# A key's decay to its block's end by a scan from the right, and the scores in two matmuls per chunk

## The chip, the cores and the metric

The kernel runs on one core of a Trainium2 chip. Its time is the device time of one execution, in microseconds: the median of three runs is 2411.07 us (2410.68 to 2414.14). The profiled execution took 2410.45 us, of which the trace spans 2408.7 us.

## The reference

One decoder layer over a prompt of 2048 tokens with 16 meta tokens ahead of it, and over 8 sample sequences of one token each. Half of the mixing width is a gated linear recurrence with four heads of 128 keys and 128 values, the other half a 31-tap depthwise convolution; a squared-ReLU MLP follows. What the change touches is the recurrence of the prompt, computed chunk by chunk:

```
b = jnp.cumsum(logf, axis=3)          # log of the gates, summed from the block's start
b_end = b[:, :, :, -1:, :]
q_dec = q * jnp.exp(b)
k_inv = k * jnp.exp(-b)               # divided by the decay from the block's start
k_end = k * jnp.exp(b_end - b)        # decay from the key to the block's end
scores = jnp.where(causal, einsum('bnhtd,bnhsd->bnhts', q_dec, k_inv), 0.0)
o_intra = einsum('bnhts,bnhsv->bnhtv', scores, v)
ds = einsum('bnhsd,bnhsv->nbhdv', k_end, v)
s_next = exp(b_end) * s + ds ;  o = o_intra + einsum(q_dec, s)
```

## The kernel before

The prompt is worked through in four quarters (q = 0 to 3) of 512 tokens; quarter 0 also carries the 16 meta tokens and the 8 sample tokens. Phase 1 is a list of units, each one 128-column piece of a weight matrix times the quarter's activations: 24 input units per quarter ("in": per head the gate f, the query q, the output gate g and the value v, and the pairs a, b of the convolution) and 8 output units ("out"). A unit of quarter 0 is 48 matmuls of 260 or 268 columns, of the other quarters 24 of 512. Each product is three matmuls of high and low parts (mm3, L645). Phase 2 is the MLP, in two halves of the tokens. TensorE (PE) runs the units one after the other; a unit's epilogue (in_epilogue, L1270) takes its result out of PSUM. In quarter 0 that is a VectorE multiply by a row of norms, so a unit can start only when the epilogue of the unit two before it has freed its banks.

Everything else is background work, written as generators that a planner interleaves with the units (Background, L159). The planner keeps a model of each engine's time (Proxy, L112: a scan costs 60 + 3.0 ns per element, a reciprocal 75 + 6.4, a tensor-tensor operation 155 + 1.045) and lets a step be written into its engine's queue once the model says that its inputs are ready; a VectorE step may be written when the engine's model is less than 600 ns ahead (HORIZON, L160). All that stands between two `yield` lines is written in one go. The order that results is fixed when the program is built, and each engine then follows its queue.

The background work that matters here is `hgrn` (L887), once per quarter and head, 16 times in all, one at a time (hgate). It works on four chunks of 128 tokens, each of two blocks of 64. A forward scan makes B, the decay from each block's start; the reciprocal of all of B makes I; keys times I, times the first block's decay, give the key operand K of the scores and, times the second block's decay, the operand I of the state update. QS, Q and K are the operands of the score matmuls; the tile scT takes the masked scores; vn and KPn are the transposed values and keys; Sch and Sst hold the states. KPn is used again for the normed output, whose transposes end the head's work on PE. Other background work beside it: the convolution's taps (conv_part, L1092; a tap is a VectorE operation on a PSUM bank, or a ScalarE multiply and a GpSimd add), the preparation of the next quarter's inputs (x_pair, L393; row_bc, L370, its broadcast through the tile dg), the sample rows' convolution (conv_sample, L1134) and state update (hgrn_sample, L1018). All instructions carry line 154, that of the helper which records them, so groups are read by their tiles.

Of the kernel before, what the change touches and what calls it, by code (L numbers as in the profile page):

```python
# [13 lines left out]
ALU = mybir.AluOpType  # L14
AX = mybir.AxisListType

P = 128
# [4 lines left out]
QT = SEQ // NQ  # L22
META = 16
# [204 lines left out]
def tile_hybrid_step(  # L228
# [6 lines left out]
    V, S, G, T, SP = (Proxy(e, n, model) for e, n in (  # L235
        (nc.vector, "dve"), (nc.scalar, "act"), (nc.gpsimd, "pool"), (nc.tensor, "pe"), (nc.sync, "dma")))
# [45 lines left out]
    ps = psum.tile([P, 8, 512], F32, name="ps")  # L282
# [18 lines left out]
    def keep(n):  # L301

        if kcols[0] + n > 88:
            kcols[0] = 0
        a = kept[:, kcols[0]:kcols[0] + n]
        kcols[0] += n
        return a
# [34 lines left out]
    def bank1():  # L342
        got = yield from bank(1)
        return got[0]
# [441 lines left out]
    with tc.manual_schedule():  # L786
# [4 lines left out]
        with ExitStack() as p1:  # L791
            mix_p = p1.enter_context(tc.tile_pool(name="mix", bufs=1))

            def mt(shape, name, dt=F32):
                return mix_p.tile(shape, dt, name=name)
# [7 lines left out]
                     for t, n in (("F", 2), ("K", 2), ("Q", 2), ("Sg", 4), ("V", 2))}  # L803
            B_t = mt([P, QT + META], "B")
            I_t = mt([P, QT + META], "I")
            d1 = mt([P, QT], "d1")
            QS = mt([P, 4, P], "QS")
            vn = mt([P, 4, P], "vn")
            KPn = mt([P, 4, P], "KPn")
# [77 lines left out]
            def hgrn(q, h, tl):  # L887
                Ft, Kt, Qt, Sg, Vt = tl["F"], tl["K"], tl["Q"], tl["Sg"], tl["V"]
                yield from take1(hgate)
                p0 = META if q == 0 else 0  # L890
                Fp = Ft[:, p0:p0 + QT]
                Bp = B_t[:, p0:p0 + QT]
                Ip = I_t[:, p0:p0 + QT]
                Kp, Qp = Kt[:, p0:p0 + QT], Qt[:, p0:p0 + QT]
                yield "dve"
                V.tensor_copy(d1[:, 0:QT:64], Fp[:, 0:QT:64])
                V.memset(Fp[:, 0:QT:64], 0.0)
                V.tensor_tensor_scan(Bp, Fp, d1, 0.0, ALU.mult, ALU.add)
                if q == 0:
                    V.tensor_tensor_scan(B_t[:, 0:META], Ft[:, 0:META], mone, 1.0, ALU.mult, ALU.mult)  # L900
                n = p0 + QT
                V.reciprocal(I_t[:, 0:n], B_t[:, 0:n])
                yield "pe"
                bv = yield from bank1()
                for j in range(4):
# [6 lines left out]
                def pr(t):  # L912
                    return t.rearrange("p (j u t) -> p j u t", j=4, u=2)

                kv, qv, iv, bvw = pr(Kp), pr(Qp), pr(Ip), pr(Bp)
                EA = bvw[:, :, 0, 63:64]
                EB = bvw[:, :, 1, 63:64]
                EAb = EA.to_broadcast([P, 4, 64])
                EE, IA = keep(4), keep(4)
                V.tensor_tensor(Kp, Kp, Ip, ALU.mult)  # L920
                V.tensor_copy(IA, iv[:, :, 0, 63])
                V.tensor_tensor(kv[:, :, 0], kv[:, :, 0], EAb, ALU.mult)
                if q == 0:
                    V.scalar_tensor_tensor(out=Kt[:, 0:META], in0=Kt[:, 0:META], scalar=B_t[:, META - 1:META],
                                           in1=I_t[:, 0:META], op0=ALU.mult, op1=ALU.mult)
                V.tensor_tensor(Ip.rearrange("p (j t) -> p j t", j=4), Kp.rearrange("p (j t) -> p j t", j=4),
                                EB.to_broadcast([P, 4, P]), ALU.mult)
                yield "dve"
                V.tensor_tensor(EE, EA.rearrange("p j o -> p (j o)"), EB.rearrange("p j o -> p (j o)"), ALU.mult)
                V.tensor_tensor(qv[:, :, 0], qv[:, :, 0], bvw[:, :, 0], ALU.mult)  # L930
                V.tensor_tensor(QS[:, :, 64:P], qv[:, :, 1], bvw[:, :, 1], ALU.mult)
                V.tensor_tensor(QS[:, :, 0:64], qv[:, :, 0], IA.unsqueeze(2).to_broadcast([P, 4, 64]), ALU.mult)
                V.tensor_tensor(qv[:, :, 1], QS[:, :, 64:P], EAb, ALU.mult)
                yield "pe"
                bk = yield from bank1()
# [13 lines left out]
                bs = yield from bank1()  # L949
                for j in range(4):  # L950
                    T.matmul(ps[:, bs, j * P:(j + 1) * P], lhsT=Kp[:, j * P:(j + 1) * P], rhs=QS[:, j],
                             start=True, stop=True)
                yield "dve"
                V.copy_predicated(scT, mask.unsqueeze(1).to_broadcast([P, 4, P]),
                                  ps[:, bs, :].rearrange("p (j t) -> p j t", j=4))
# [314 lines left out]
            def in_epilogue(u, q, t, c):  # L1270
# [31 lines left out]
                else:  # L1302
# [17 lines left out]
                    if t == "v":  # L1320
                        bg.add(hgrn(q, c, dict(cur)), 2)
                        if q == 0 and c == HEADS - 1:
                            bg.add(hgrn_sample_norm(), 1.7)
# [76 lines left out]
            for u in range(2, n_phase1):  # L1400
                kind, q, t, c, pi = plan[u]
# [308 lines left out]
```

## Time and profile before

| | us |
|---|---|
| median of three runs | 2411.07 |
| profiled execution | 2410.45 |
| its span in the trace | 2408.7 |
| PE busy | 2343.8 (97%) |
| VectorE (DVE) busy | 1086.2 (45%) |
| ScalarE (ACT) busy | 685.7 (28%) |
| GpSimd (POOL) busy | 579.1 (24%) |

PE is busy nearly all of the span, and its waits are short; 45% for VectorE is a mean over phase 1, where it is nearly full in places, and phase 2, where it is nearly idle. So the averages say little on what a change inside phase 1 is worth: that is read from the waits of PE, and from stretches of 25 us, whose PE clock column says what part of the full clock (2.4 GHz) the engine was granted; a stretch below 1.00 holds some time at 1.2 GHz.

### The profile page before, as it was taken

Reading aid. Unit: us, or ns where it says so; the run is one execution under the profiler, and the core shown is the slowest. Engines: PE = TensorE matmul, PEld = TensorE weight load, DVE = VectorE, ACT = ScalarE, POOL = GpSimd, SP = SyncE. Lnnn points to the kernel's source line nnn. Section 1 sums busy time; section 2 is a strip of 40 time slices with the busy share of each in tenths; the row PEclk is TensorE's granted clock in tenths of the full one; section 3 lists DMA queues with packets and bytes.
Section 4 is the critical chain, followed back from the end, with each engine's and each line's share of the span. In section 5 each row is a group of like instructions: output and inputs, shape, how many; then the busy total and the mean of one; then the engine's idle time right before and its main releaser. Section 6 shows DMA issues by size and latency. Waiting matters only on the chain.

```text
span 2408.7 us, 31153 instructions
## 1 busy us (share of the span) xinstructions
PE 2343.8 (97%) x13000; PEld 2097.1 (87%) x13000; DVE 1086.2 (45%) x1454; ACT 685.7 (28%) x1244; POOL 579.1 (24%) x383
## 2 busy tenths in 40 slices
PE   8988899999999989999999999999999999999998
PEld 8987788978888878999999999999888888888887
DVE  6887968478469342522323323325422222222224
ACT  6544645454355232211211211213200100100112
POOL 4653525455256023222222222211000000000000
PEclk9998999999999999999999999999999999999999
DMA  9774555944654668444444444449522222222222
GB/s 309 232 231 140 175 192 189 319 158 174 232 197 168 213 226 302 149 136 149 140 132 144 144 131 140 146 135 338 186 105 88 97 96 88 105 88 104 89 89 104
DMA packets 159218, 396.25 MB, mean 165 GB/s; under 512 B 8772, under 2 KB 107657, under 8 KB 125278
## 3 DMA queue, kind: packets, MB, share of 16 engines
q1 hardware_dynamic: 158934, 394.00, 48.1%
q8 instruction: 102, 1.67, 0.3%
q14 instruction: 38, 0.31, 0.0%
q10 hardware_dynamic: 144, 0.26, 0.0%
HBM read 265.91 MB, written 128.79 MB: 164 GB/s over the span
## 4 chain that ended last, share of the span: by engine, by line
PE 78%; DVE 4%; issue 1%; ACT 1%; POOL 1%; DMA 0%; POOLq 0%; ACTq 0%; DVEq 0%
PE ps L154 78%; DVE ps L154 2%; DVE I L154 1%; DVE act L154 1%; POOL scr L154 0%; DMA wsp<-kw 0%; ACT scr L154 0%; DVE kept L154 0%; DVE B L154 0%; DVE K L154 0%; DVE scr L154 0%; DVE stat L154 0%; DVE QS L154 0%; DVE d L154 0%; ACT F L154 0%
## 5 line engine op out<-in xcount | busy, mean ns | idle before, releaser
L154 PE MATMUL ps<-act,wsp 128*128 128x512 f32 (+5 forms) x7704 | 1502.6, 354 | 13.4 <-DVE F L154 9.3
L154 PEld LDWEIGHTS ps<-act,wsp 128*128 128x128 f32 x7704 | 1284.3, 191 | 174.5 <-DVE F L154 7.1
L154 PE MATMUL ps<-hid,wsp 128*128 128x344 f32 (+4 forms) x3864 | 713.9, 346 | 0.9 <-DMA wsp<-kw 0.9
L154 PEld LDWEIGHTS ps<-hid,wsp 128*128 128x128 f32 x3864 | 646.5, 188 | 63.4 <-DVE kept L154 0.7
L154 POOL TENSOR_TENSOR wsp<-raw,wsp 128x1024 fp32r<-128x1024 f32 (+1 forms) x98 | 234.9, 2396 | 630.0 <-ACT wsp L154 579.5
L154 DVE TENSOR_TENSOR acc<-ps,acc 128x1032 f32<-128x1032 f32 (+5 forms) x160 | 162.1, 1013 | 470.4 <-PE ps L154 470.3
L154 DVE TENSOR_TENSOR xn<-xn 128x1032 f32<-128x1032 f32 (+3 forms) x68 | 79.9, 1176 | 520.7 <-ACT hid L154 520.7
L154 ACT ACTIVATE xn<-ps 128x1032 f32<-128x1032 f32 (+5 forms) x74 | 69.2, 935 | 849.6 <-PE ps L154 846.9
L154 POOL TENSOR_TENSOR scr<-scr 128x512 f32<-128x512 f32 x177 | 239.5, 1353 | 148.5 <-ACT scr L154 131.2
L154 POOL TENSOR_TENSOR kept<-stat,mhalf 128x4 f32<-128x4 f32 (+4 forms) x48 | 38.5, 804 | 900.8 <-DVE stat L154 900.2
L154 DVE SCALAR_TENSOR_TENSOR ps<-glu,cw,ps 128x512 f32<-128x512 f32 x287 | 216.1, 753 | 8.0
L154 ACT ACTIVATE wsp<-raw 128x1024 fp32r<-128x1024 f32 (+1 forms) x98 | 101.5, 1036 | 298.2 <-PE ps L154 222.3
L154 DVE TENSOR_TENSOR hid<-xn,hid 128x1032 fp32r<-128x1032 f32 (+3 forms) x68 | 135.5, 1993 | 2.3
L154 ACT ACTIVATE scr<-glu,cw 128x512 f32<-128x512 f32 x193 | 129.0, 714 | 0.5 <-DVE glu L154 0.5
L154 ACT ACTIVATE junk<-ps 128x128 bf16<-128x128 f32 (+3 forms) x100 | 38.3, 383 | 121.0 <-PE ps L154 105.2
L154 DVE TENSOR_TENSOR scr<-ps,scr 128x512 f32<-128x512 f32 x48 | 32.8, 684 | 85.3 <-DMA scr<-xscr 60.8
L154 ACT ACTIVATE hid<-xn 128x1032 fp32r<-128x1032 f32 (+3 forms) x68 | 69.0, 1015 | 2.2
L154 POOL TENSOR_TENSOR fg<-fg 128x512 f32<-128x512 f32 x28 | 37.7, 1346 | 82.1 <-ACT fg L154 82.1
L154 DVE RECIPROCAL I<-B 128x512 f32<-128x512 f32 (+1 forms) x16 | 54.0, 3378 | 0.5
L154 DVE TENSOR_TENSOR act<-scr,act 128x512 fp32r<-128x512 f32 (+1 forms) x31 | 27.8, 897 | 46.1 <-ACT act L154 46.1
L154 ACT ACTIVATE scr<-ps,vec 128x128 f32<-128x128 f32 (+1 forms) x68 | 25.3, 454 | 28.3 <-PE ps L154 28.3
L154 ACT ACTIVATE fg<-scr 128x512 f32<-128x512 f32 x32 | 20.0, 628 | 45.2 <-DVE scr L154 41.6
(185 smaller groups left out, 1139.7 us busy)
## 6 DMA issues: line engine op xcount, KB each, us to landing
wsp<-kw SPq DMA_DIRECT2D x167, 1024.0 KB, 4.8
kw<-wsp SPq DMA_DIRECT2D x96, 1024.0 KB, 5.7
raw<-in_w_up_dram SPq DMA_DIRECT2D x32, 512.0 KB, 6.4
raw<-in_w_down_dram SPq DMA_DIRECT2D x32, 512.0 KB, 6.0
raw<-in_w_in_dram SPq DMA_DIRECT2D x24, 512.0 KB, 8.0
out_dram<-xn SPq DMA_DIRECT2D x18, 512.0 KB, 4.6
scr<-xscr SPq DMA_DIRECT2D x32, 256.0 KB, 7.0
hscr<-scr SPq DMA_DIRECT2D x32, 256.0 KB, 6.4
```

Source lines behind the costliest of these rows:

```text
L154: return fn(*args, **kw)
```

## The change

The reciprocal of whole rows is gone. Instead a second scan runs over the gates from the right and puts into I the decay from each key to its own block's end (the tile d1, one column longer, restarts it with ones at each block's end). The keys of the first block times that are the first half of K; the keys of the second block times that go into the second half of I; the first half of I is the first half of K times the second block's decay. Only the eight decays at the block ends are inverted (IE), and quarter 0's 16 meta tokens. The second half of K now holds bare keys until a new multiply overwrites it with QS times the inverse decay of the second block, as a query operand. A chunk's scores are then two matmuls: the one of 128 by 128 as before, and behind it one of 64 by 64 that writes the second block's scores over the lower right quarter. A `yield "dve"` stands between the two scans. The planner's costs are as before.

```diff
-            d1 = mt([P, QT], "d1")
+            d1 = mt([P, QT + 1], "d1")
...
-                V.tensor_tensor_scan(Bp, Fp, d1, 0.0, ALU.mult, ALU.add)
+                V.tensor_tensor_scan(Bp, Fp, d1[:, 0:QT], 0.0, ALU.mult, ALU.add)
+                yield "dve"
+                V.memset(d1[:, 64:QT + 1:64], 1.0)
+                V.tensor_tensor_scan(Ip[:, ::-1], Ft[:, p0 + 1:p0 + QT + 1][:, ::-1], d1[:, 1:QT + 1][:, ::-1], 0.0,
+                                     ALU.mult, ALU.add)
                 if q == 0:
                     V.tensor_tensor_scan(B_t[:, 0:META], Ft[:, 0:META], mone, 1.0, ALU.mult, ALU.mult)
-                n = p0 + QT
-                V.reciprocal(I_t[:, 0:n], B_t[:, 0:n])
+                    V.reciprocal(I_t[:, 0:META], B_t[:, 0:META])
...
-                EE, IA = keep(4), keep(4)
-                V.tensor_tensor(Kp, Kp, Ip, ALU.mult)
-                V.tensor_copy(IA, iv[:, :, 0, 63])
-                V.tensor_tensor(kv[:, :, 0], kv[:, :, 0], EAb, ALU.mult)
+                EE, IE = keep(4), keep(8)
+                V.tensor_tensor(kv[:, :, 0], kv[:, :, 0], iv[:, :, 0], ALU.mult)
+                V.tensor_tensor(iv[:, :, 1], kv[:, :, 1], iv[:, :, 1], ALU.mult)
...
-                V.tensor_tensor(Ip.rearrange("p (j t) -> p j t", j=4), Kp.rearrange("p (j t) -> p j t", j=4),
-                                EB.to_broadcast([P, 4, P]), ALU.mult)
+                V.tensor_tensor(iv[:, :, 0], kv[:, :, 0], EB.to_broadcast([P, 4, 64]), ALU.mult)
                 yield "dve"
+                V.reciprocal(IE, Bp[:, 63:QT:64])
                 V.tensor_tensor(EE, EA.rearrange("p j o -> p (j o)"), EB.rearrange("p j o -> p (j o)"), ALU.mult)
+                ie = IE.rearrange("p (j u) -> p j u", u=2)
                 V.tensor_tensor(qv[:, :, 0], qv[:, :, 0], bvw[:, :, 0], ALU.mult)
                 V.tensor_tensor(QS[:, :, 64:P], qv[:, :, 1], bvw[:, :, 1], ALU.mult)
-                V.tensor_tensor(QS[:, :, 0:64], qv[:, :, 0], IA.unsqueeze(2).to_broadcast([P, 4, 64]), ALU.mult)
+                V.tensor_tensor(QS[:, :, 0:64], qv[:, :, 0], ie[:, :, 0:1].to_broadcast([P, 4, 64]), ALU.mult)
+                V.tensor_tensor(kv[:, :, 1], QS[:, :, 64:P], ie[:, :, 1:2].to_broadcast([P, 4, 64]), ALU.mult)
                 V.tensor_tensor(qv[:, :, 1], QS[:, :, 64:P], EAb, ALU.mult)
...
                     T.matmul(ps[:, bs, j * P:(j + 1) * P], lhsT=Kp[:, j * P:(j + 1) * P], rhs=QS[:, j],
                              start=True, stop=True)
+                    T.matmul(ps[64:P, bs, j * P + 64:(j + 1) * P], lhsT=iv[:, j, 1],
+                             rhs=kv[:, j, 1], start=True, stop=True)
```

Since the planner's model sees other costs, the order of all of phase 1 behind the first scan changes with it. Three places follow, in the order in which the engines' queues hold the instructions.

The first is VectorE at the first head of quarter 0. F_115 is that head's gate, F_116 the next head's, whose row is the epilogue that frees PSUM for a unit of PE; rows `ps<-glu,cw,ps` are taps of the convolution. Before:

```order
L154 COPY d_129<-F_115 128x8
L154 MEMSET F_115 128x8 [waits DVE_49]
L154 SCALAR_TENSOR_TENSOR B<-F_115,d_129 128x512 [waits DVE_49]
L154 SCALAR_TENSOR_TENSOR B<-F_115,ones 128x16
L154 RECIPROCAL I<-B 128x528 [waits DVE_49]
L154 TENSOR_TENSOR F_116<-ps,fg 128x536 [waits PE_49]
```

Now:

```order
L154 COPY d_129<-F_115 128x8
L154 MEMSET F_115 128x8 [waits DVE_49]
L154 SCALAR_TENSOR_TENSOR B<-F_115,d_129 128x512 [waits DVE_49]
L154 MEMSET d_129 128x8 [waits DVE_49]
L154 SCALAR_TENSOR_TENSOR I<-F_115,d_129 128x512 [waits DVE_49]
L154 SCALAR_TENSOR_TENSOR B<-F_115,ones 128x16
L154 RECIPROCAL I<-B 128x16 [waits DVE_49]
L154 TENSOR_TENSOR F_116<-ps,fg 128x536 [waits PE_49]
```

The epilogue keeps its place behind the scans; the long reciprocal ahead of it has become a memset, a second scan and a reciprocal of 16 columns.

The second is VectorE at the second head of quarter 0, where `xn<-xn,cw` and `aux<-xn` are the sample rows' convolution, scT the head's masked scores and Sch and Sst its states. Before:

```order
L154 COPY xn_91<-glu 128x8
L154 TENSOR_TENSOR xn_91<-xn_91,cw 128x248 [waits DVE_49,Activation_49]
L154 TENSOR_REDUCE aux<-xn_91 128x8 [waits DVE_49]
L154 TENSOR_TENSOR aux<-aux,vec 128x32 [waits DVE_49]
L154 SCALAR_TENSOR_TENSOR ps<-glu,cw,ps 128x512
L154 COPY_PREDICATED scT<-mask,ps 128x512 [waits PE_49]
L154 SCALAR_TENSOR_TENSOR ps<-glu,cw,ps 128x512 [waits DVE_49] x5
L154 SCALAR_TENSOR_TENSOR Sch<-Sch,kept,ps 128x128 [waits Activation_49]
```

Now:

```order
L154 SCALAR_TENSOR_TENSOR ps<-glu,cw,ps 128x512 [waits DVE_49] x6
L154 COPY_PREDICATED scT<-mask,ps 128x512 [waits PE_49,Activation_49]
L154 SCALAR_TENSOR_TENSOR ps<-glu,cw,ps 128x512 [waits DVE_49] x3
L154 TENSOR_TENSOR Sg_123<-ps,fg 128x520 [waits DMAHW0_49,PE_49]
L154 SCALAR_TENSOR_TENSOR xn_90<-xn_91,smp,xn_90 128x128 [waits DMAHW3_49,DMAHW6_49,DMAHW2_49,Activation_49]
L154 SCALAR_TENSOR_TENSOR xn_90<-xn_91,smp,xn_90 128x128 [waits Activation_49] x7
L154 SCALAR_TENSOR_TENSOR Sch<-Sch,kept,ps 128x128 [waits PE_49,Activation_49]
L154 SCALAR_TENSOR_TENSOR Sch<-Sch,kept,ps 128x128 [waits DVE_49] x2
L154 SCALAR_TENSOR_TENSOR Sst<-Sch,kept,ps 128x128 [waits DVE_49]
L154 COPY xn_93<-glu 128x8 [waits DMAHW1_49]
L154 TENSOR_TENSOR xn_93<-xn_93,cw 128x248 [waits DVE_49]
L154 TENSOR_REDUCE aux<-xn_93 128x8 [waits DVE_49]
```

The sample rows' convolution, four rounds of copy, multiply and reduce, stood ahead of scT and now stands behind the head's states; six taps stand ahead of scT.

The third is PE at the first head's scores. Before:

```order
L154 MATMUL ps<-act,wsp_87 128x268 x18
L154 MATMUL ps<-act,wsp_88 128x268 x4
L154 MATMUL ps<-act,wsp_88 128x268 [waits Pool_49]
L154 MATMUL ps<-act,wsp_88 128x268
L154 MATMUL ps<-QS,K_117 128x128 [waits Activation_49]
L154 MATMUL ps<-QS,K_117 128x128 x3
```

Now:

```order
L154 MATMUL ps<-act,wsp_89 128x268
L154 MATMUL ps<-ident,V_125 16x128
L154 MATMUL ps<-ident,K_117 16x128
L154 MATMUL ps<-act,wsp_89 128x268 x24
L154 MATMUL ps<-QS,K_117 128x128 [waits DVE_49]
L154 MATMUL ps<-K_117,I 64x64
```

The head's scores stand in an earlier unit (wsp_89 here is the value unit of the second head, wsp_87 and wsp_88 the units a and b that come after it), and a 64x64 matmul follows each of the four.

## Rows read from the trace of the kernel before

**Rows 1.** The page: engines over the span; the clock in 40 slices, tenths.

```profile
PE 2343.8 (97%) x13000; PEld 2097.1 (87%) x13000; DVE 1086.2 (45%) x1454; ACT 685.7 (28%) x1244; POOL 579.1 (24%) x383
...
PEclk9998999999999999999999999999999999999999
```

**Rows 2.** Stretches of 25 us: busy us (instructions) per engine, PE clock, DMA share, GB/s.

```profile
75.00:100.00 25.00, 20.80 (x150) 20.10 (x150) 23.53 (x29) 10.57 (x16) 13.71 (x9) 0.86 0.62 187
...
150.00:175.00 25.00, 23.55 (x178) 23.23 (x177) 20.47 (x22) 14.37 (x25) 17.73 (x11) 0.90 0.56 174
175.00:200.00 25.00, 14.03 (x71) 12.74 (x70) 24.02 (x45) 9.40 (x33) 10.01 (x7) 0.66 0.47 147
200.00:225.00 25.00, 22.04 (x155) 21.07 (x154) 20.21 (x29) 11.25 (x19) 10.48 (x8) 0.93 0.51 181
...
575.00:600.00 25.00, 25.00 (x114) 20.37 (x113) 24.04 (x35) 13.19 (x24) 13.48 (x11) 1.00 0.54 203
```

**Rows 3.** Waits of PE by the engine waited for: us in total, times, longest.

```profile
PE ps L154 <- ACT KPn L154: 12.0, 3, 9.1
PE ps L154 <- DVE F L154: 9.3, 3, 3.7
PE ps L154 <- DVE scT L154: 7.5, 2, 7.2
```

**Rows 4.** Timeline, quarter 0, first head: start, us, instruction, [idle before it, releaser].

```profile
76.49 3.10 POOL L154 TENSOR_TENSOR wsp<-raw,wsp 128x1024 fp32r<-128x1024 f32 x1 [0.16 <-ACT wsp L154]
77.33 2.31 DVE L154 TENSOR_TENSOR_SCAN B<-F,ones 128x16 f32<-128x16 f32 x1
...
79.67 3.45 DVE L154 RECIPROCAL I<-B 128x528 f32<-128x528 f32 x1
...
83.04 0.65 DVE L154 TENSOR_TENSOR F<-ps,fg 128x536 f32<-128x536 f32 x1
...
83.84 1.64 PE L154 MATMUL ps<-act,wsp 128*128 128x260 f32 x6 [2.64 <-DVE F L154]
```

**Rows 5.** Timeline, VectorE, the first head of quarter 1, which nothing disturbs.

```profile
304.24 1.23 DVE L154 TENSOR_TENSOR_SCAN B<-F,d 128x512 f32<-128x512 f32 x1
...
305.50 3.35 DVE L154 RECIPROCAL I<-B 128x512 f32<-128x512 f32 x1
...
310.32 0.69 DVE L154 TENSOR_TENSOR I<-K,B 128x512 f32<-128x512 f32 x1
310.93 0.16 DVE L154 TENSOR_TENSOR kept<-B 128x4 f32<-128x4 f32 x1
311.00 0.42 DVE L154 TENSOR_TENSOR Q<-Q,B 128x256 f32<-128x256 f32 x1
...
311.34 0.42 DVE L154 TENSOR_TENSOR QS<-Q,B 128x256 f32<-128x256 f32 x1
```

**Rows 6.** Timeline, PE: narrow and full matmuls; a record is one pass.

```profile
280.61 0.60 PE L154 MATMUL ps<-ident,aux 128*8 128x128 f32 x4
281.04 1.06 PE L154 MATMUL ps<-QS,K 128*128 128x128 f32 x8
281.86 0.47 PE L154 MATMUL ps<-act,wsp 128*128 128x512 f32 x1
...
285.70 0.48 PE L154 MATMUL ps<-small 16*128 16x128 f32 x2
...
330.83 1.84 PE L154 MATMUL ps<-smp,xn 128*128 128x2 f32 x16
...
476.89 0.73 PE L154 MATMUL ps<-ones,fg 128*128 128x2 f32 x17
```

**Rows 7.** Timeline, quarter 0, second head: the scores and what follows them.

```profile
170.96 1.13 PE L154 MATMUL ps<-QS,K 128*128 128x128 f32 x8 [1.45 <-DVE QS L154]
...
182.05 0.71 DVE L154 COPY_PREDICATED scT<-mask,ps 128x512 f32<-128x512 int32 x1
...
182.82 0.79 PE L154 MATMUL ps<-small 16*128 16x128 f32 x2 [7.18 <-DVE scT L154]
```

## The prediction

> **What bounds the kernel now.** I read the page first. PE is busy for 97% of the span and its clock is full in nearly every slice [rows 1], so time can be won or lost in three ways: matmuls that PE has more or fewer of, waits of PE, and the stretches in which it is granted 1.2 instead of 2.4 GHz. The list of PE's waits came next: the three largest entries that the change can touch are 12.0 us for KPn, 9.3 us in three waits for F, and 7.5 us for scT [rows 3]. The stretches of 25 us say where: in quarter 0 PE is busy 20.80, 23.55, 14.03 and 22.04 of 25 us, at clocks of 0.86, 0.90, 0.66 and 0.93. At 575 us, with the later quarters, it is busy 25.00 of 25 at a clock of 1.00, while VectorE is busy 24.04 [rows 2]. So the change is decided in quarter 0, some 75 to 310 us. In the later quarters whatever VectorE gains or loses is hidden by PE, which has no wait there to give back. The timeline last, to see what each wait stands behind.
>
> **The change part by part.** The sum starts from the profiled run, 2410.45 us (2408.7 in the span and 1.75 around it); the median is 0.6 us above.
>
> *VectorE's work per head.* Removed: the reciprocal, keys times I, the copy, the decay of the first half and the 512-wide I, which together run from 305.50 to 310.93 in an undisturbed head, 5.43 us. Added: a scan like the first (304.24 to 305.50, 1.26 us), four multiplies of 256 columns at 0.34 (311.00 to 311.34), a memset and a reciprocal of eight columns. The last two are not in the trace; the smallest operation takes a slot of 0.07 us (310.93 to 311.00) and a duration of 0.16, so 0.3 for both [rows 5]. Together 2.9, or 2.5 us less per head and 40 us over 16 heads. Twelve of the heads lie in the later quarters under PE's full stretches and count as nothing; if that cover were gone, each would be worth at most its 2.5 us. A scan that reads from right to left is not in the trace either; I take the forward one's 1.26, and as bounds that and the reciprocal's 3.35 [rows 5]. At 3.35 the gain of the next two items is gone.
>
> *The waits for F, −6.3 us.* In quarter 0 the next head's gate must leave PSUM before PE can start the unit two further on. That copy stands behind everything that the recurrence writes into VectorE's queue in one go: at the first head behind the reciprocal, from 79.67 until the copy's 83.04, 3.37 us, and PE waits 2.64 [rows 4]. The order of the changed kernel leaves the copy there, but the 3.37 become a memset, a scan and a reciprocal of 16 columns, 0.1 + 1.26 + 0.1: the copy comes 1.9 us sooner. At the third head the order puts it between the two scans, so that it waits for less still. Three waits of 9.3 in all [rows 3], the first of 2.64, the longest 3.7: each loses 1.9, at most what it is, so 5.7 if all lose the same and up to 7.5 where one goes altogether; I take 6.3 and keep 0 and 9.3 as ends.
>
> *The clock, −6 us.* Each of the three waits falls into a stretch with a lower clock: 0.86, 0.90 and 0.93 of 25 us are 3.5, 2.5 and 1.75 us of lost PE work [rows 2]. A wait of 1.45 us cost nothing of the kind: the eight passes behind it took 1.13 us against 1.06 in a stretch without a wait [rows 6, 7]. What remains of the F waits is 0.7 to 1.8 us. Of the 7.75 I take 6; the ends are 0 and 7.75.
>
> *The second score matmul, +10.0 us.* 64 matmuls (four chunks, 16 heads), each of two passes as the old ones (128 records for 64 matmuls). The trace has no 64x64. A full pass takes 0.10 to 0.11 us: eight begin at 281.04 and the next work at 281.86. A pass of 128 weight columns with only two moving columns still takes 0.115 (1.84 over 16); one of eight weight columns and two moving, 0.043 (0.73 over 17) [rows 6]. So wide weights cost as much as wide data, and half of both should take half, 0.056. Behind the two short passes the next chunk's 128 weight columns are only half covered, 0.055 more, for three of four chunks. That is 64 x 2 x 0.056 + 48 x 0.055 = 9.8, taken as 10. PE is the bound, so all of it counts. Ends: 128 x 0.043 = 5.5, and 128 x 0.24 = 30.7 with the dearest narrow pass, that of 16 rows (0.48 over two) [rows 6].
>
> The Trainium skill has a rule against this part: TensorEngine Tiling (Array Packing), section Tiling Modes, says that changing the tiling mode, not merely the tile, drains TensorE. By it each of the 64 would cost as the third rival has it; the eight-column transposes, which are narrow tiles too, show no such drain.
>
> *The second head's scores, −5 us.* PE waits 7.18 us at the meta tokens' product because the masked copy into scT only ran at 182.05, behind the sample rows' convolution on VectorE [rows 7]. That stretch has the lowest clock, 0.66, or 8.5 us lost [rows 2]. In the changed order the convolution stands behind the head's states; ahead of scT are six taps, at 0.75 to 0.8 each some 4.6 us, against about 5 us of PE work, so a wait of 2 to 4 us may stay. That is −4 in waits and about −4 in clock. Against it: at the first head the broadcast rows for the next inputs (tile dg) now come behind the masked copy, and the head's steps on PE stand closer together; I put +3 for new waits there. The ends are wide, since an order has no times: −17 (7.18 and 8.5 and a little) to +9 (as much new waiting as the F waits are now).
>
> *What stays.* The longest wait for KPn, 9.1 us [rows 3], belongs to the last head of quarter 0, whose norm waits for taps on VectorE and adds on GpSimd. The new order has six taps and a conv start ahead of that step, where six taps and a small subtraction stood, and nearly the same work of PE; I leave it as it is. Behind the end of phase 1 PE's order is the old one.
>
> The sum: 2410.45 + 10.0 − 6.3 − 6 − 5 = 2403.2, so 2403 us, 0.3% below the median.
>
> **Rivals.** *Waits merely change their place* (25%). The F waits and their clock go, and the new order makes as many waits as it removes: 2410.45 + 10 − 12.3 = 2408, no change that can be told. For it: the planner's costs did not change, and what makes PE wait in quarter 0 is that they do not know of delays such as the next rival's. Against it: the worst wait has a cause, the sample rows' convolution, that leaves its place.
>
> *The second scan is held up by GpSimd* (9%), slower. A scan of 16 columns took 2.31 us: it began at 77.33 and ended at 79.64, just behind a GpSimd subtraction that ended at 79.59 [rows 4]. The reciprocal kept its usual time. If every new scan in quarter 0 is held for as long, 2.2 us, then 0.1 + 1.26 + 2.2 + 0.1 is 3.7 and no shorter than the reciprocal; F waits and clock stay, the head's steps come as late as before and the new order gains nothing: 2410.45 + 10 = 2420. It decides from a mean hold of 1.9 us. Against it: GpSimd is busy in only half of that stretch (13.71 of 25) [rows 2].
>
> The Trainium skill states this, SBUF — State Buffer, section Who interferes with whom: a VectorE instruction with two SBUF inputs contends with a GpSimd one that reads SBUF, one with a single input does not, and the loser blocks for the whole instruction. The 2.31 us agree. By that rule the change trades a single-input reciprocal for two-input scans and multiplies.
>
> *The narrow matmul is dear* (8%), slower: each switch between 128 and 64 columns empties PE, so that a pass costs the 0.24 us of the 16-row product [rows 6]: 30.7 in place of 10, 2424. Against it: four transposes with eight weight columns run from 280.61 to 281.04, 0.11 each, with no gap on either side.
>
> *Quarter 0 comes out nearly free of waits* (14%): in addition to the forecast, the second head loses its whole 7.18 and 8.5 and no new wait arises at the first: 2410.45 + 10 − 12.3 − 16 = 2392.
>
> That the change does not do what it says can be left out: the order shows the reciprocal gone and 64 matmuls more.
>
> **How the numbers follow.** Forecast 44%, own range 2396 to 2410; rivals 25, 9, 8 and 14%. Range 2388 to 2420: below, the last rival with a matmul at its lower end; above, the hold of the scan; the dear matmul lies outside. About 0.2%, 5 us, is what a measurement of this kernel tells from no change: faster is below 2406, slower above 2416. Faster: 38 of the forecast's 44, 14 of the last rival, 5 of the second-named 25 (the case of moved waits), 57%. Same: 6 of the forecast, 17 of the moved waits, 2 of the held scan, 25%. Slower: 3 of the moved waits, 7 of the held scan, 8 of the dear matmul, 18%.
>
> **What would show it.** In the profile after: no RECIPROCAL of 512 columns; 16 more scans of 1.2 to 1.4 us; VectorE some 35 to 40 us less busy; PE's wait for F below 4 us in total; clocks in the stretches from 75 to 225 us nearer to 1; scT no longer among PE's long waits; KPn still with one of about 9; 128 records of 64x64 with 0.05 to 0.12 us from one to the next; PE some 10 us busier. The prediction is wrong if F still costs 9 us, if a pass of 64 takes over 0.2 us, or if new waits of 10 us or more stand in quarter 0.

## The result and the profile after

| | before | after |
|---|---|---|
| median, us | 2409.73 (2408.32 to 2414.14, 6 runs) | 2428.18 (2425.84 to 2429.98, 6 runs) |
| profiled execution, us | 2410.45 | 2427.06 |
| PE busy, us | 2343.8 | 2366.4 |
| VectorE busy, us | 1086.2 | 1045.3 |
| PE's waits, sum of the list, us | 56.6 | 50.3 |

The ratio is 1.0074 (95% interval 1.0061 to 1.0087): the changed kernel is slower by 18 us where 7 us less were forecast. Three things have to be read off: VectorE did get lighter by 41 us, PE waits 6 us less, and PE itself works longer.

First the engines, the line of the page that answers to [rows 1].

```profile
PE 2366.4 (98%) x13128; PEld 2110.1 (87%) x13128; DVE 1045.3 (43%) x1494; ACT 684.4 (28%) x1240; POOL 578.0 (24%) x379
```

Next the stretches of 25 us, with the columns of [rows 2], and behind those the two in which something went wrong that was not foreseen.

```profile
75.00:100.00 25.00, 21.54 (x160) 20.22 (x160) 23.41 (x34) 10.87 (x16) 17.15 (x11) 0.93 0.67 204
150.00:175.00 25.00, 23.97 (x179) 22.77 (x179) 22.06 (x37) 12.20 (x33) 13.76 (x9) 0.93 0.62 208
175.00:200.00 25.00, 18.01 (x121) 17.28 (x120) 23.00 (x37) 12.09 (x26) 14.89 (x10) 0.86 0.58 195
200.00:225.00 25.00, 25.00 (x162) 21.79 (x161) 15.77 (x38) 11.17 (x25) 10.31 (x8) 1.00 0.52 184
275.00:300.00 25.00, 10.61 (x49) 8.56 (x48) 21.92 (x32) 12.79 (x36) 11.81 (x10) 0.66 0.19 63
750.00:775.00 25.00, 21.98 (x94) 17.17 (x93) 24.36 (x31) 10.66 (x18) 14.39 (x11) 0.89 0.34 125
```

The last two of these in the kernel before:

```profile
275.00:300.00 25.00, 17.87 (x98) 14.45 (x96) 22.48 (x37) 14.79 (x36) 14.06 (x12) 0.90 0.42 147
750.00:775.00 25.00, 24.14 (x125) 19.74 (x124) 23.84 (x36) 12.91 (x28) 16.89 (x14) 1.00 0.45 164
```

From 75 to 225 us the clock came up as forecast: 0.86, 0.90, 0.66 and 0.93 have become 0.93, 0.93, 0.86 and 1.00. But the worst stretch of quarter 0 is now at 275 us, where PE is busy 10.61 of 25 us, and at 750 us there is a stretch below full clock that the kernel before did not have. PE's waits, to be held against [rows 3]:

```profile
PE ps L154 <- ACT KPn L154: 19.2, 2, 14.4
...
PE ps L154 <- DVE K L154: 3.0, 1, 3.0
PE ps L154 <- DVE I L154: 2.8, 1, 2.8
PE ps L154 <- DVE d L154: 2.2, 1, 2.2
...
PE ps L154 <- DVE F L154: 0.6, 1, 0.6
```

F fell from 9.3 to 0.6 us and the wait for scT is gone. The row for `d` is really the third head's F: the timeline, VectorE and PE there.

```profile
190.07 1.23 DVE L154 TENSOR_TENSOR_SCAN B<-F,d 128x512 f32<-128x512 f32 x1
191.21 0.69 DVE L154 TENSOR_TENSOR F<-ps,fg 128x536 f32<-128x536 f32 x1
191.86 0.07 DVE L154 MEMSET d<- 128x8 f32 x1
...
191.96 4.67 PE L154 MATMUL ps<-act,wsp 128*128 128x260 f32 x24 [2.17 <-DVE d L154]
```

The epilogue stands between the two scans, as the order had it, and ends just when PE goes on; the memset behind it only came last by the profile. So the F waits are 0.6 + 2.2 = 2.8 us, 6.5 less. New are 3.0 for K, 2.8 for I, and 7.2 more for KPn.

Where PE works longer is seen at the first head's scores, timeline of PE, with one of its weight loads (PEld) for later (start, duration; a record is a pass):

```profile
96.72 0.38 PE L154 MATMUL ps<-QS,K 128*128 128x128 f32 x2
97.03 0.19 PEld L154 LDWEIGHTS ps<-K,I 128*64 128x64 f32 x2
97.03 0.33 PE L154 MATMUL ps<-K,I 128*64 128x64 f32 x2
97.29 0.49 PE L154 MATMUL ps<-QS,K 128*128 128x128 f32 x2
97.71 0.33 PE L154 MATMUL ps<-K,I 128*64 128x64 f32 x2
...
99.32 1.75 PE L154 MATMUL ps<-act,wsp 128*128 128x268 f32 x12
```

Read the starts, not the durations, which overlap. From one chunk's first pass to the next chunk's it is now 97.97 − 97.29 = 0.68 us, and the four chunks take 99.32 − 96.72 = 2.60 us where the undisturbed block of [rows 6] took 0.81. That is 1.79 us per head. Over all 16 heads the score blocks, from first pass to the work behind, take 42.5 us after and 13.3 us before (worked out from the starts of all score passes in the two traces): 29.2 us, against 10 forecast.

The books of the two profiled executions: +29.2 for the blocks, −6.3 of waits, and the stretches below full clock from 75 to 325 us, which lost 24.0 us before and 15.5 now, less 2.8 in the new one at 750 us, −5.7. Together +17.2; the two differ by 16.6. The clock's part is rough: a stretch is counted as lost by its clock also where PE was idle (14.39 of the 25 us at 275 us), so it gives the most that can have been lost, and that the sums meet to 0.6 us is in part luck.

### The profile page after: what moved, and what is told of

It is laid out like the page before. It is cut to its first block, busy times and chain, and to the rows that moved or that the text cites. A ratio compares the mean times of both kernels' runs of the same rounds, so it can differ in the third digit from the quotient of the medians.

```text
span 2425.3 us, 31434 instructions
## 1 busy us (share of the span) xinstructions
PE 2366.4 (98%) x13128; PEld 2110.1 (87%) x13128; DVE 1045.3 (43%) x1494; ACT 684.4 (28%) x1240; POOL 578.0 (24%) x379
## 4 chain that ended last, share of the span: by engine, by line
PE 89%; DVE 5%; DMA 2%; POOL 1%; ACT 1%; issue 1%; SPq 0%; POOLq 0%; ACTq 0%; DVEq 0%
PE ps L154 89%; DVE ps L154 2%; DMA raw<-in_w_in_dram 1%; POOL scr L154 1%; DVE act L154 1%; ACT scr L154 0%; DMA scr<-xscr 0%; POOL wsp L154 0%; DVE I L154 0%; DVE glu L154 0%; DVE scr L154 0%; DVE xn L154 0%; DMA xn<-in_x_prompt_dram 0%; DVE stat L154 0%; DVE B L154 0%
## 5 line engine op out<-in xcount | busy, mean ns | idle before, releaser
L154 POOL TENSOR_TENSOR wsp<-raw,wsp 128x1024 fp32r<-128x1024 f32 (+1 forms) x98 | 237.9, 2428 | 627.0 <-ACT wsp L154 584.3
L154 POOL TENSOR_TENSOR scr<-scr 128x512 f32<-128x512 f32 x173 | 234.3, 1355 | 145.0 <-ACT scr L154 133.9
L154 DVE COPY_PREDICATED scT<-mask,ps 128x512 f32<-128x512 int32 x16 | 11.8, 740 | 59.3 <-PE ps L154 59.3
L154 PE MATMUL ps<-QS,K 128*128 128x128 f32 x128 | 30.2, 318 | 3.0 <-DVE K L154 3.0
```

The costliest lines, as they stand in the source:

```text
L154: return fn(*args, **kw)
```

## Experiments

In the first two "held" kernels below (`one_held`, `held_recip`) the planner is charged as in the changed kernel, so that the order of every engine stays the changed kernel's; `grouped`, `wide64`, `low64` and `tr64` keep it too, and `before_64` keeps the order of before. `held_last` and `held_all` are charged in the same way, but what they hold back changes the order. Each kernel was timed beside runs of the kernel before, whose median was 2411.6, 2411.0 and 2411.7 us in the three groups.

### What the second matmul costs: without it, and alone

`one_held` takes the 64 narrow matmuls away from the changed kernel, `before_64` adds them to the kernel before.

```diff
-                V.tensor_tensor(kv[:, :, 1], QS[:, :, 64:P], ie[:, :, 1:2].to_broadcast([P, 4, 64]), ALU.mult)
+                V.tensor_tensor(kv[:, :, 1], iv[:, :, 1], ie[:, :, 1:2].to_broadcast([P, 4, 64]), ALU.mult)
...
-                    T.matmul(ps[64:P, bs, j * P + 64:(j + 1) * P], lhsT=iv[:, j, 1],
-                             rhs=kv[:, j, 1], start=True, stop=True)
+                    model.op("pe", 214.0)
```

> The changed kernel with one score matmul per chunk: the second half of K is the second half of I (key times the decay to its block's end) times the inverse decay of the block, so the 128x128 matmul covers all four quarters, and the 64 matmuls of 64x64 are left out. The multiply stands where the old one stood, and the planner still charges the 64 matmuls, so every engine's order is the changed kernel's. Theory S (each switch between 128 and 64 columns holds PE up, and nothing else went wrong): in the changed kernel's trace a chunk's scores take 0.677 us from one to the next against 0.222 for two passes of 128 before, so 64 x 0.455 = 29 us go: 2399 us, within 4 for waits that shift. Rival W (the narrow matmul costs the 10 us forecast, and the rest of the loss is waits made by the new order): 2418 us, with the same order's waits still there.

Measured: 2400.1 us (ratio to before 0.9952, 0.9940 to 0.9964). A score block (a head's scores, from the first pass to the work behind them) takes 0.81 us again; the long waits are the changed kernel's (KPn still 19.2), the whole list is 3.9 us longer (54.2).

```profile
96.38 1.05 PE L154 MATMUL ps<-QS,K 128*128 128x128 f32 x8
97.19 1.73 PE L154 MATMUL ps<-act,wsp 128*128 128x268 f32 x12
```

```diff
                     T.matmul(ps[:, bs, j * P:(j + 1) * P], lhsT=Kp[:, j * P:(j + 1) * P], rhs=QS[:, j],
                              start=True, stop=True)
+                    T._eng.matmul(ps[64:P, bs, j * P + 64:(j + 1) * P], lhsT=Kp[:, j * P + 64:(j + 1) * P],
+                                  rhs=QS[:, j, 64:P], start=True, stop=True)
```

> The kernel before, with a 64x64 matmul added behind each of its 64 score matmuls, which writes the same scores of the second block again; the planner is not told, so all orders are those of before. Theory S: the whole price of the second matmul without anything else of the change, 64 x 0.455 = 29 us, less what falls into PE's waits of quarter 0 (at most 4 x 1.8): 2410 + 22 to 29 = 2432 to 2439 us. Rival W: 10 us, 2420 us.

Measured: 2434.2 us (1.0094, 1.0081 to 1.0107), 22.6 more than before. Its blocks sum to 41.9 us, 28.6 more, so 6 us came back elsewhere. The waits do not show where: KPn fell from 12.0 to 9.6 and scT from 7.5 to 5.9, but others grew, and the list is as long as before (56.5 against 56.6). The clock may: from 75 to 325 us the stretches lost 17.2 us in place of 24.0, counted as above. So the blocks cost 28 to 29 us in either order, of which 22.6 show in the time here and 28 in the changed kernel's order, and what is left of the change without them is a gain of 11.5.

### What in it costs: the switch of tile

`grouped` puts the four narrow matmuls behind the four wide ones.

```diff
+                for j in range(4):
                     T.matmul(ps[64:P, bs, j * P + 64:(j + 1) * P], lhsT=iv[:, j, 1],
                              rhs=kv[:, j, 1], start=True, stop=True)
```

> The changed kernel with the four 64x64 matmuls of a head behind its four 128x128 ones, so that the array changes its tile twice per head and not eight times; all else, the orders too, unchanged. Theory S (the switch costs): 7 x 0.111 + 0.205 + 7 x 0.107 + 0.152 + 0.102 = 1.99 us per head against 4 x 0.677 = 2.71, so 0.72 less in each of 16 heads, 11.6 in all: 2416.5 us. Rival N (the 64x64 pass is slow in itself, or because it writes over what the matmul just ahead of it wrote in the same bank): nothing changes but the small part of the second kind, 2426 to 2428. Rival W (waits made by the order): 2428.

Measured: 2410.4 us (0.9998, 0.9989 to 1.0007), 17.7 less than the changed kernel, more than was expected. Timeline of PE, first head:

```profile
98.66 1.05 PE L154 MATMUL ps<-QS,K 128*128 128x128 f32 x8
99.64 0.68 PE L154 MATMUL ps<-K,I 128*64 128x64 f32 x8
100.25 1.77 PE L154 MATMUL ps<-act,wsp 128*128 128x268 f32 x12
```

Eight wide passes take 0.98 up to the first narrow one, 0.09 more than 8 x 0.111. The eight narrow ones take 0.61, in which, by the starts of the single passes, six follow each other at 0.058, the first takes 0.107 and the last 0.152. I had taken 0.107 for the price of each; it is that of the first behind a switch. 0.058 is what the forecast had (0.056): the pass was priced right, the switch was not in the sum.

`wide64` keeps the alternation and takes the narrow tile away.

```diff
-                    T.matmul(ps[64:P, bs, j * P + 64:(j + 1) * P], lhsT=iv[:, j, 1],
+                    T.matmul(ps[:, bs, j * P + 64:(j + 1) * P], lhsT=Ip[:, j * P:(j + 1) * P],
                              rhs=kv[:, j, 1], start=True, stop=True)
```

> The changed kernel with the second score matmul made 128 weight columns wide (both halves of I), 64 moving columns, at the same place and into the same bank; its result fills the upper right quarter too, so the second block's scores against the first block's keys are not the reference's. The orders are unchanged. Theory S: no switch of tile, so a pass takes between half and all of a 128x128 pass, 0.056 to 0.112 us, 7 to 14 us for 128 passes in place of 29: 2406 to 2413 us. Rival N (writing over the bank just written, or a short moving side, is what costs): 2425 to 2428 us.

Measured: 2410.9 us (1.0001, 0.9991 to 1.0011). (The upper right quarter gets the reference's scores after all: the second block's decay in I and its inverse in the query operand cancel.)

```profile
96.38 0.33 PE L154 MATMUL ps<-K,I 128*128 128x64 f32 x2
96.55 0.44 PE L154 MATMUL ps<-QS,K 128*128 128x128 f32 x2
96.83 0.33 PE L154 MATMUL ps<-K,I 128*128 128x64 f32 x2
97.00 0.44 PE L154 MATMUL ps<-QS,K 128*128 128x128 f32 x2
```

Same alternation, same bank, same overwriting, as short a moving side: a chunk takes 97.00 − 96.55 = 0.45 us, 0.22 over one matmul alone and 0.23 below the changed kernel. That excludes overwriting and the short moving side as the cause of the rest, and leaves the width of the tile. The 0.22 is more than the 0.116 of two short passes: by the starts of the single passes, the second short one holds PE 0.112 us where 0.058 is its price in a row, and the first full one behind it 0.165 where the others take 0.111.

`low64` moves the narrow tile to the other half of the columns.

```diff
-                    T.matmul(ps[64:P, bs, j * P + 64:(j + 1) * P], lhsT=iv[:, j, 1],
+                    T.matmul(ps[0:64, bs, j * P + 64:(j + 1) * P], lhsT=iv[:, j, 1],
```

> The changed kernel with each 64x64 matmul writing to the upper half of the partitions (0 to 63) and not to the lower, so that it uses the left and not the right half of the array's columns; the scores of the second block are then in the wrong quarter. Theory S (the switch to 64 columns costs, wherever the tile lies): 2.60 us per score block as in the changed kernel, 2425 to 2430 us. Rival P (it is the tile's place away from column 0 that costs; the eight-column transposes, which lie at 0, cost nothing): about 1.7 us per block as with wide weights, 2409 to 2413 us.

Measured: 2428.0 us (1.0073, 1.0056 to 1.0089), 2.60 us per block: where the tile lies makes no difference.

`tr64` makes the narrow operation a transpose, the kind from which the prediction had concluded that narrow tiles are switched to free of charge.

```diff
-                    T.matmul(ps[64:P, bs, j * P + 64:(j + 1) * P], lhsT=iv[:, j, 1],
-                             rhs=kv[:, j, 1], start=True, stop=True)
+                    model.op("pe", 214.0)
+                    T._eng.transpose(ps[0:64, bs, j * P:(j + 1) * P], iv[:, j, 1], ident)
```

> The changed kernel with each 64x64 matmul replaced by a transpose of the same 64 columns of I into the chunk's upper half, so the scores are not the reference's. Its tile has 64 columns as the old one's, but it is a transpose, as the eight-column operations were that showed no gap in the kernel before. Theory T (a transpose switches free of charge, an ordinary matmul does not, and I read the price off the wrong kind): passes of 0.11 with no gap, 16 x 0.111 = 1.78 us per score block, 0.82 less than in the changed kernel, 13 us: 2415 us, 2412 to 2418. Rival E (eight columns are free and 64 are not, transpose or no): 4 x (0.677 + 2 x 0.05) = 3.1 us per block, 2435 us.

Measured: 2403.7 us (0.9968, 0.9957 to 0.9979), better than either theory's figure, since a transpose is one pass where I had counted two: a block takes 1.24 us, not 1.78.

```profile
98.27 0.38 PE L154 MATMUL ps<-QS,K 128*128 128x128 f32 x2
98.49 0.27 PE L958 MATMUL ps<-ident,I 128*64 128x128 f32 x1
98.60 0.39 PE L154 MATMUL ps<-QS,K 128*128 128x128 f32 x2
98.71 0.11 PEld L958 LDWEIGHTS ps<-ident,I 128*64 128x64 f32 x1
98.82 0.27 PE L958 MATMUL ps<-ident,I 128*64 128x128 f32 x1
```

The starts run 98.27, 98.49, 98.60, 98.82: every pass 0.11, no gap into or out of the 64 columns. With the same 64 columns an ordinary matmul costs a gap on both sides and a transpose none. The weight loads show the same: here the load of the 64 columns starts at 98.71, a pass ahead of its transpose at 98.82; in the changed kernel it starts at 97.03, together with its matmul. So at the ordinary matmul's edge nothing is loaded ahead. Two things stay open: whether the late load is the cause of the gap or goes along with it, and why a transpose is spared, for which it may be enough that it does not run as a narrow tile at all. No run separates these.

### What the reciprocal cost: put back as dead work

```diff
+                V._eng.reciprocal(Ip, Bp)
                 V.memset(d1[:, 64:QT + 1:64], 1.0)
                 V.tensor_tensor_scan(Ip[:, ::-1], Ft[:, p0 + 1:p0 + QT + 1][:, ::-1], d1[:, 1:QT + 1][:, ::-1], 0.0,
```

> The kernel with one score matmul per chunk in the changed kernel's order (2400.1 us), with the reciprocal of all of B (512 columns, 3.35 us) put back between the two scans as dead work that the reverse scan then overwrites; the planner is not told, so all orders stay. Theory F (the reciprocal's place ahead of the epilogue and of the head's operands is what made PE wait in quarter 0): the waits for F, d and I, 6.0 us together, grow by up to 3.35 at each of three heads, and their stretches lose clock again: +4 to +14, 2404 to 2414 us, all of it in quarter 0; the twelve later heads cost nothing. Rival O (the order alone set those waits, and 3.35 us of VectorE disappear beside PE everywhere): 2399 to 2402 us.

Measured: 2411.9 us (1.0008, 0.9997 to 1.0019), 11.8 more than `one_held` (some 4 us either way, by the two intervals). Theory F holds, but for one later head that now waits (1.2 us for I at 534.21). Quarter 0 and one later stretch:

```profile
75.00:100.00 25.00, 21.48 (x163) 20.83 (x162) 24.54 (x34) 10.09 (x15) 15.48 (x10) 0.93 0.66 200
...
200.00:225.00 25.00, 22.48 (x151) 20.82 (x152) 22.04 (x34) 13.76 (x28) 14.15 (x9) 0.93 0.50 185
...
750.00:775.00 25.00, 22.86 (x115) 18.77 (x114) 24.32 (x35) 13.78 (x23) 17.52 (x13) 1.00 0.44 166
```

PE's waits grow by 6.4 us to 60.6 (F 4.0, two waits), and its clock from 75 to 325 us loses 22.5 us in place of 15.5. The result stands where the kernel before stands, with VectorE as busy as there (1085.2 us against 1086.2): with the reciprocal's time given back, the new order, for all its other waits, is worth nothing that can be measured.

### What the order is worth, and the wait for KPn

`one_free` is `one_held` without the line `model.op("pe", 214.0)`, so the planner counts the matmuls that are there.

> One score matmul per chunk, and the planner is told so (no charge for the 64 that are gone), so that the order of phase 1 is a new one. Theory S: the score blocks stay at 0.81 us a head, and only waits and clock differ: 2400 us, within 8, since the waits of quarter 0 come to 34 us before and 26 now. Rival O (the order decides more than the work): more than 8 us away from 2400.

Measured: 2398.2 us (0.9946, 0.9933 to 0.9959): the same within the intervals, though the long wait of quarter 0 now stands at a transpose for ScalarE's scr (14.4 us) and not at KPn.

That wait is read from GpSimd's queue. Quarter 0, last head, in the changed kernel:

```profile
281.09 0.79 DVE L154 TENSOR_SCALAR stat<-stat 128x4 f32<-128x4 f32 x1
...
282.19 9.34 POOL L154 TENSOR_TENSOR scr<-scr 128x512 f32<-128x512 f32 x7 [0.34 <-ACT act L154]
...
291.49 1.02 POOL L154 TENSOR_TENSOR kept<-stat,mhalf 128x4 f32<-128x4 f32 x1
292.54 1.14 ACT L154 ACTIVATE KPn<-ps,kept 128x128 f32<-128x128 f32 x4 [6.70 <-POOL kept L154]
292.96 0.95 PEld L154 LDWEIGHTS ps<-ident,KPn 128*128 128x128 f32 x4 [14.48 <-ACT KPn L154]
292.96 1.25 PE L154 MATMUL ps<-ident,KPn 128*128 128x128 f32 x4 [14.39 <-ACT KPn L154]
```

The sums of squares are ready at 281.9, and the power of the norm, 1 us of work, waits behind seven adds of the convolution. In the kernel before there were four:

```profile
295.22 5.29 POOL L154 TENSOR_TENSOR scr<-scr 128x512 f32<-128x512 f32 x4 [1.84 <-ACT scr L154]
...
300.47 1.02 POOL L154 TENSOR_TENSOR kept<-stat,mhalf 128x4 f32<-128x4 f32 x1
```

9.34 − 5.29 = 4.05 of the 5.3 us by which this wait grew. The next kernels let the planner write no such adds between a head's squares and its power.

```diff
         if e == "side":
-            return r <= now and max(t["act"], t["pool"]) < now + self.SPARE
+            return not self.hold and r <= now and max(t["act"], t["pool"]) < now + self.SPARE
...
+                bg.hold = q == 0 and h == 3
                 yield "act"
                 ss = sc(4)
...
                 rr = yield from rsqrt(ss, 4, 1.0 / P)
+                bg.hold = False
```

> One score matmul per chunk in the changed kernel's order, but the planner writes no GpSimd adds from the squares of quarter 0's last head until that head's power is in GpSimd's queue. In the changed kernel seven adds (9.34 us) run ahead of that power, which ScalarE's KPn and then PE (14.4 us) wait for. Theory K: the wait falls by the 9.3 us to about 5, and the stretch with clock 0.66 gives back 4 to 8: 2400 - 9.3 - 6 = 2385 us, 2381 to 2391. Rival L (the wait's other releasers are as late: taps on VectorE, the sums that the adds feed): 2396 to 2401 us.

Measured: 2397.0 us (0.9944, 0.9931 to 0.9956), 3.1 below `one_held`, less than the two intervals together, and in the range of rival L, not of theory K: it can't be told from no gain. The wait itself did what theory K said:

```profile
276.57 0.16 DVE L154 TENSOR_SCALAR stat<-stat 128x4 f32<-128x4 f32 x1
...
276.81 1.02 POOL L154 TENSOR_TENSOR kept<-stat,mhalf 128x4 f32<-128x4 f32 x1 [5.63 <-DVE stat L154]
...
278.28 1.25 PE L154 MATMUL ps<-ident,KPn 128*128 128x128 f32 x4 [4.22 <-ACT KPn L154]
```

14.4 became 4.2 us. But the order behind it is another, and quarter 1 got waits that were not there (2.35 for dg at 341.79, 3.30 for KPn at 368.10), so PE's waits as a whole fell by 6.8, not 10.2. A gain at one place was partly given back a quarter later.

`held_all` sets `bg.hold = True` for every head.

> The same hold of GpSimd's adds for all 16 heads, not only the last of quarter 0. Theory K: as that one, and the third head's wait for KPn (4.8 us at 182 us) shrinks too, by 2 to 4 with some clock: 2381 us, 2374 to 2388. Rival L: the adds that are held back come due at the convolutions' ends and PE waits there, in quarter 0 or at the end of phase 1: 2392 to 2404 us.

Measured: 2389.1 us (0.9910, 0.9897 to 0.9923), 11 below `one_held`, 1 us above theory K's range and 3 below rival L's; PE's waits are 38.8 us in place of 54.2. (The wait at 182 us, which the expectation gives to the third head, is the second's.) `free_all` is the same with the planner's count of `one_free`.

> The version with one score matmul per chunk, the planner told so, and GpSimd's adds held back in front of the power of every head's norm. The planner-told order alone came to 2398.2 us, the hold to 2389.1 in the other order. Theory K: the hold is worth 8 to 11 us here too: 2388 us, 2384 to 2394. Rival O (what it is worth is a matter of the one order): 2395 to 2402 us.

Measured: 2384.1 us (0.9890, 0.9875 to 0.9905), 14 below `one_free`, as theory K had it and 3 more. It computes what the changed kernel computes, with one score matmul per chunk, and beats both kernels, the one before by 1.1%. How much of that the hold alone would give the kernel before, no run shows.

## Why the prediction was wrong, step by step

*The failed step: the second score matmul, +10 forecast, 28 measured.* The forecast reckoned that half the width and half the data take half the time and that only a weight load shows behind them. The half was right (0.058 us a pass, in `grouped`); missing was what PE loses each time an ordinary matmul of 64 columns follows one of 128 or is followed by it, 0.23 us per chunk (`wide64` against the changed kernel), 14.7 over 64 chunks. Most of the other 4 us is a term that was counted once and came twice: the forecast had 0.055 for the full pass behind two short ones, and in `wide64` the second short pass is held up by as much. The third rival had this mechanism and a time of 2424, near the measured 2428, and was given 8%. Its 0.24 us a pass was taken from another edge, that of 16 rows; that it comes so near what a pass cost here, 0.23 (0.455 us more per chunk, for two passes), is luck as far as the runs show. It was talked down with four transposes of eight columns that stand without a gap; `tr64` shows that a transpose has none at 64 columns either, so the witness was of the wrong kind. The right witness stood in the rows that the sum used: behind 128-column matmuls with two moving columns came 16 ordinary matmuls of eight columns [rows 6]. By the starts of single passes the last full one holds the engine 0.181 us where the others take 0.112, the narrow ones follow at 0.025, the last of them takes 0.095, and the first big pass behind them 0.338 in place of 0.234. I divided the row's 0.73 us by its 17 passes, and the switch was spread thin.

The Trainium skill's rule, TensorEngine Tiling (Array Packing), section Tiling Modes, that changing the mode drains TensorE and changing the tile within it does not, agrees in its first half with the ordinary matmuls here: 2.60 us a block at either place of the 64-column tile, 1.70 with 128 columns. That a change of the tile alone costs nothing, no run here shows.

*The reciprocal and F, −6.3 and −6 forecast.* Right. F fell by 6.5 us, its two remaining waits counted together, and `held_recip` prices the reciprocal at 11.8 us against 12.3. The clock's share alone is less sure: the three stretches that the forecast named got back 4.25 of its 7.75 us, and these are counts over whole stretches, with PE's idle time in them.

*The second head's scores and the new order, −5 forecast.* Wrong in the sum, right in the part: scT's 7.2 us are gone, but the same head waits 4.8 us for its norm (182.21), and the last head waits 5.3 us more. `held_recip`, which has the reciprocal's time and the new order and no narrow matmul, stands 0.9 us above the kernel before (interval of its ratio −0.03% to +0.19%): the first rival, waits that change their place, is what happened to this term.

*KPn, forecast to stay.* It grew from 9.1 to 14.4. The forecast had counted the taps ahead of that step on VectorE and compared PE's work; GpSimd's queue, where the order shows seven adds ahead of the power, it did not count.

*The twelve later heads, forecast to cost nothing.* In eleven of them no step of the head stands in PE's list of waits. In quarter 3, at 768 us, one does, through the contention that the prediction had named for the scans:

```profile
765.11 4.08 POOL L154 TENSOR_TENSOR scr<-scr 128x512 f32<-128x512 f32 x3 [0.18 <-ACT scr L154]
765.14 1.52 DVE L154 TENSOR_TENSOR QS<-Q,kept 128x256 f32<-128x256 f32 x1
766.58 1.48 DVE L154 TENSOR_TENSOR K<-QS,kept 128x256 f32<-128x256 f32 x1
...
768.12 0.49 PE L154 MATMUL ps<-QS,K 128*128 128x128 f32 x2 [3.02 <-DVE K L154]
```

Multiplies of 256 columns that take 0.42 us undisturbed [rows 5] take 1.5 beside GpSimd's adds, and PE waits 3.0 us.

*The held second scan (9%).* It happened and did not decide. In quarter 0 the four new scans took 3.09, 1.99, 1.23 and 1.98 us, a mean hold of 0.85 where the rival needed 1.9. At the first head the scan took nearly as long as the reciprocal that it replaced, and ended at 81.10, 1.09 us behind the GpSimd subtraction that ran until 80.01:

```profile
76.74 3.27 POOL L154 TENSOR_TENSOR wsp<-raw,wsp 128x1024 fp32r<-128x1024 f32 x1
...
78.01 3.09 DVE L154 TENSOR_TENSOR_SCAN I<-F,d 128x512 f32<-128x512 f32 x1
...
82.18 6.01 PE L154 MATMUL ps<-act,wsp 128*128 128x260 f32 x48 [0.63 <-DVE F L154]
```

Still PE waits 0.6 for F and not 2.6, since the first 16-column scan, held for 2.3 us before, went through in 0.16. The mean of the 16 new scans is 1.66 us, of the forward ones 1.58 (1.42 before). The Trainium skill's rule, SBUF — State Buffer, section Who interferes with whom, that VectorE instructions with two SBUF inputs and GpSimd's reads exclude each other, agrees with these rows and with those at 765 us.

With 28 in place of 10 and 0 in place of −5 the forecast's own sum gives 2410.45 + 28 − 6.3 − 6 = 2426; the profiled execution took 2427.

## What to carry to other kernels

Before a narrow matmul is priced by its size, look for a place in the trace where an operation of the same kind, not a transpose, follows a wide one, and read the starts of the single passes at the edge, not a mean over the group. Where PE is the bound, keep matmuls of one tile width together, or fold the correction into an operand (here one multiply of the same length) and keep one matmul. And when a planner reorders, count what stands ahead of a waited-for step in every engine's queue: for a 1 us operation behind seven adds PE waited 14.4 us, longer than for all the F waits that were aimed at (9.3).

## What the runs showed of the hardware that was not expected

- A change from 128 to 64 columns and back costs ordinary fp32 matmuls 0.23 us per round trip more than a tile of 128 columns with the same moving side (a chunk of 0.68 us against 0.45), at either half of the columns; grouped, twice per head, it costs 16 x (1.59 − 0.81) = 12.5 us with all passes, alternating 29.
- A transpose of 64 columns between matmuls of 128 costs its one pass, 0.11 us, and no gap.
- A scan from right to left takes 1.22 us undisturbed, as the forward one does, and up to 3.09 beside GpSimd.
